# A decoder layer on one core: gates, scan output, half of h, queries, keys and probabilities transposed by DMA instead of on TensorE, and the weights of those stages loaded through GpSimd's queue

## The chip, the cores and the metric

The kernel runs on one core of one Trainium2 chip. The metric is the device time of one execution in microseconds; the number to beat is the median of three runs of the kernel before.

## The reference

One layer of a hybrid decoder for 256 tokens of width 2048, in float32. With n = RMSNorm of the stream at each place:

```
h = x + 1/2 * SwiGLU_1(RMSNorm(x))                     w_gu 2048 x 11264, w_down 5632 x 2048
P = RMSNorm(h) @ W_in                                  columns: u 2048 | v 2048 | z 2048 | x 2048 | B 1024 | C 1024 | dt 32
a = gelu(u) * (W_s RMSNorm(gelu(v)) + b)               causal within 128 tokens, 4 groups
m = RMSNorm(SSD scan(conv(x, B, C), dt) * silu(z))     32 heads of 64, state 128, chunks of 128
h = h + concat([a, m]) @ W_out                         4096 x 2048
h = h + softmax(q k^T / sqrt(512)) v @ W_o             4 heads; q from RMSNorm(h), k and v from RMSNorm(mem), 256 memory tokens
h = h + 1/2 * SwiGLU_2(RMSNorm(h))
out = RMSNorm(h)
```

Every matrix product on TensorE contracts over the partitions, so each activation that is produced with tokens on the partitions has to be transposed to features on the partitions before it can be the operand of the next product.

## The kernel before, in words

**Precision.** A float32 product is made of three products of a faster type: each operand is split into a high part (a cast on ScalarE) and a low part (the difference, on VectorE), and high*high, high*low and low*high are added up in PSUM. So each weight tile of 1 MB (256 rows by 1024 columns, four blocks of 128 by 512) is loaded into one of three `raw` buffers, cast to `hi` (L169, three buffers), subtracted to `lo` (L177, two buffers), and multiplied.

**Pieces.** A product runs over pieces of 256 contracted rows; one piece is one *step*. A piece of kind C takes 24 matmuls of 512 columns. A piece of kind S uses a scheme of the Strassen-Winograd kind with seven block products instead of eight, 21 matmuls, and more VectorE work (sums of the weight blocks, two splits). Its weights are loaded by three transfers (L151 once, L154 twice), those of a C piece by one (L140). Strings such as "CCSCSCSC" say which piece is of which kind; the first of `OUT_KINDS` holds the pieces of the gating operand `at`, the second those of the scan operand `mt`, and the output projection names for each half of its columns how they are multiplied. A slot of 8 KB per partition (12 in `big`) holds two C pieces or one S piece.

**Stages in order.** FFN 1 (up to about 640 us, its last down projection to about 700); the mix stage: B, C and x columns with features on the partitions (`proj_feat`), then v, u and z columns with tokens on the partitions (`proj_tok`), with the scan worked in between; the output projection in two halves of 1024 columns, 16 pieces each (`add_sum`, 1198 to 1365 us); queries for heads 0-1 and 2-3, keys, values (`heads`, 8 pieces for each pair of heads), the attention of each head (`attend`, `turn_probs`, `weigh`); the output of the attention (`add_sum`); FFN 2 from about 1750 us.

**Order of work.** TensorE keeps the order of the program. Jobs that prepare the next stage are put off by `later(fn, by)` and called at the first step at which they fall due; while all eight PSUM banks are taken (between the first and the last S piece), only jobs marked `bankless` are called. The other engines and the queues are ordered by a planner that goes by the code's order among what it reckons to be ready; `issue_after` (in `behind`, `in_turn`) holds some instructions in order on ScalarE and VectorE.

**Transposes.** Most operands are transposed on TensorE (`transpose`, L77): a block of 128 by 128 against the identity into a PSUM bank, eight for a chunk of 256 tokens by 512 columns, then cast and subtracted from the bank (`to_operand`, `Pieces.put`, `Pieces.sums`). This is done for the gates (`ats.later`), the scan output (`mts.later` in `m_operand`), the four chunks of h for the mix stage, the attention and FFN 2 (`Normed.chunk`), queries and keys (`by_head`), and the probabilities (`turn_probs`). The hidden units of both FFNs go another way (`Pieces.turn_later`): ScalarE copies a tile into planes of 16-bit halves (L485), GpSimd's queue writes them to device memory (L487), and SyncE's queue reads them back with a transposing transfer (L491) into a tile `turned` in SBUF, of which the operand is made.

**Queues.** All weights are loaded on SyncE's queue (`load`). GpSimd's queue carries the planes, the memory tokens (`prep_mem`, L1005 and L109), the decay rows of the scan, and small loads; GpSimd itself computes the power -1/2 of each norm (L361). Each queue is worked in order: an issue that waits holds those behind it.

Of the kernel before, what the change touches and what calls it, by code (L numbers as in the profile page):

```python
# [17 lines left out]
P = 128  # L18
D = 2048
S = 256  # L20
# [27 lines left out]
def hybrid_layer(ctx: ExitStack, tc: tile.TileContext, x, xt, mem, memt, w_gu1, w_dn1, w_in, w_s, w_out,  # L48
# [12 lines left out]
    tmp = ctx.enter_context(tc.tile_pool(name="tmp", bufs=6))  # L61
# [73 lines left out]

    def load(w, r0, cs, at, fine=False):
        raw = wraw.tile([P, 2 * KP, NC], F32, name="raw")
        rows = w[r0:r0 + KP * P, :]
        if at is PLAIN and cs[1] == cs[0] + NC:
            nc.sync.dma_start(out=raw.rearrange("p (k j) n -> p k j n", j=2), in_=rows[:, cs[0]:cs[0] + 2 * NC].rearrange(  # L140
                "(k p) (j n) -> p k j n", p=P, j=2))
            return raw
        if fine:
            for (k, j), b in at.items():
                nc.sync.dma_start(out=raw[:, b, :], in_=rows[k * P:(k + 1) * P, cs[j]:cs[j] + NC])
            return raw
        for j, c in enumerate(cs):
            b, e = at[0, j], at[1, j]
            src = rows[:, c:c + NC]
            if e > b:  # L150
                nc.sync.dma_start(out=raw[:, b:e + 1:e - b, :], in_=src.rearrange("(k p) n -> p k n", p=P))  # L151
                continue
            for k, x in enumerate((b, e)):
                nc.sync.dma_start(out=raw[:, x, :], in_=src[k * P:(k + 1) * P, :])  # L154
# [210 lines left out]
    def in_turn(src, last, op):  # L365

        if not src.tensor.name.startswith("turned"):
# [6 lines left out]
    def to_operand(srcs, dst, q, c0=None, of=None):  # L374
# [13 lines left out]
        else:  # L388
            scs = [col[:, c0 + of + k:c0 + of + k + 1] for k in range(2)]
            for k in range(2):  # L390
                hi = nc.scalar.activation(dst[:, q + k, :S], ps[:, k, :], AF.Copy, scale=scs[k])
            for k in range(2):
                lo = nc.vector.scalar_tensor_tensor(out=dst[:, q + k, S:], in0=ps[:, k, :], scalar=scs[k],
                                                    in1=dst[:, q + k, :S].bitcast(F32),
                                                    op0=ALU.mult, op1=ALU.subtract)
# [19 lines left out]

    owed = []


    class Pieces(dict):
        def __init__(self, kinds, name, donor=None):  # L420

            self.kinds, self.name, self.half, self.made, self.donor = kinds, name, None, {}, donor

# [33 lines left out]
        def sums(self, dst, ps, c0=None):  # L457
            in_sbuf = ps.tensor.name.startswith("turned")
            if not in_sbuf or c0 is not None:
                a = half_k(F32, "forms").rearrange("p (f s) -> p f s", f=4)  # L460
            if in_sbuf and c0 is None:
                a = ps
            elif c0 is None:
                nc.scalar.copy(out=a, in_=ps)
            else:
                for k in range(2):
                    nc.scalar.activation(a[:, 2 * k:2 * k + 2], ps[:, 2 * k:2 * k + 2], AF.Copy,
                                         scale=col[:, c0 + k:c0 + k + 1])

            b = half_k(F32, "forms").rearrange("p (f s) -> p f s", f=4)  # L470
            in_turn(a, last_split, lambda: nc.vector.tensor_tensor(
                out=b[:, 0:2], in0=a[:, 1:2].broadcast_to([P, 2, P]), in1=a[:, 0:4:3], op=ALU.subtract))
# [8 lines left out]
        def turn_later(self, srcs, by):  # L481
            planes = dram.tile([S, 2, NC], U16, name="planes", tag="planes", bufs=2)
            for t in range(NT):
                halves = tmp.tile([P, 2 * NC], U16, name="halves", tag="t2k")
                nc.scalar.copy(out=halves.rearrange("p (b n) -> p b n", b=2),  # L485
                               in_=srcs[t].bitcast(U16).rearrange("p (n b) -> p b n", b=2))
                nc.gpsimd.dma_start(out=planes[t * P:(t + 1) * P].rearrange("p b n -> p (b n)"), in_=halves)  # L487
            for q in (0, 2):
                def fetch(q=q):
                    to = half_k(F32, "turned").rearrange("p (k s) -> p k s", k=KP)  # L490
                    nc.sync.dma_start(out=to.bitcast(U16).rearrange("p k s -> p (k s)").rearrange("p (k s) -> p k s", k=KP),  # L491
                                      in_=planes[:, :, q * P:(q + 2) * P].rearrange("s b n -> (s b) n"), transpose=True)
# [700 lines left out]
```

## Time and profile before

| | |
|---|---|
| median of 3 runs | 2431.41 us (2431.26 to 2431.83) |
| the profiled execution | 2432.23 us, span 2430.5 us |
| TensorE (PE) | busy 2419.1 us, 100% |
| TensorE weight load (PEld) | 2014.9 us, 83% |
| VectorE (DVE) | 2033.1 us, 84% |
| ScalarE (ACT) | 1351.7 us, 56% |
| GpSimd (POOL) | 59.0 us, 2% |
| granted TensorE clock | 0.999 |
| moved by DMA | 503.87 MB, mean 207 GB/s |
| SyncE's queue (q1) | 475.86 MB, 60.6% of the 16 DMA engines' span |
| GpSimd's queue (q0) | 25.12 MB, 2.8% |

A row of a group has line, engine, operation, output<-input by the program's names with shapes, the count, then busy us and mean ns of one, and behind the next bar the idle time of the engine just ahead of these instructions with what ended it. A row of a wait has who waited, for whom, the us in total, how often, and the longest. "PE" is the matrix multiplication, "PEld" the loading of its stationary operand; SPq and POOLq are the queues of SyncE and GpSimd. A matmul's duration in a row is the pipelined one; the distance from one to the next is shorter.

### The profile page before, as it was taken

The numbers are of one execution on the slowest core, as the hardware profiler recorded it, in microseconds if no ns is written. First come the engines' busy times: TensorE is split into PE (matmuls) and PEld (weight loads), VectorE is DVE, ScalarE is ACT, GpSimd is POOL, SyncE is SP. The second block draws the span as 40 slices with busy tenths as digits, with TensorE's granted clock in tenths as the row PEclk, the third lists the DMA queues.
The fourth block names the chain that finished last, engine by engine and source line by source line (L and its number), as shares of the span: only waits on it lengthen the run. The fifth ranks groups of instructions, "written<-read, shape, count | busy, mean of one in ns | idle before, by whom it ended". The sixth has DMA issues, their size and how long they took to land.

```text
span 2430.5 us, 29042 instructions
## 1 busy us (share of the span) xinstructions
PE 2419.1 (100%) x11189; PEld 2014.9 (83%) x11189; DVE 2033.1 (84%) x1943; ACT 1351.7 (56%) x1251; POOL 59.0 (2%) x112
## 2 busy tenths in 40 slices
PE   9999999999999999999999999999999999999998
PEld 7888888888888888788888888888888888888887
DVE  8999889999877777655698888778899988899997
ACT  7565446565556555435555655555556554556554
POOL 1000000000000000000000000000000000000000
PEclk9999999999999999999999999999999999999999
DMA  8767667677555555545566655555567666776774
GB/s 302 238 221 232 205 208 232 221 232 227 196 186 189 189 185 179 204 160 187 182 203 231 232 187 165 174 182 181 187 213 240 225 213 203 223 226 226 232 220 154
DMA packets 251211, 503.87 MB, mean 207 GB/s; under 512 B 62896, under 2 KB 64976, under 8 KB 250304
## 3 DMA queue, kind: packets, MB, share of 16 engines
q1 hardware_dynamic: 243552, 475.86, 60.6%
q0 software_dynamic: 6688, 25.12, 2.8%
q8 instruction: 87, 1.43, 0.2%
q10 hardware_dynamic: 832, 1.05, 0.1%
q14 instruction: 52, 0.43, 0.1%
HBM read 476.76 MB, written 13.66 MB: 202 GB/s over the span
## 4 chain that ended last, share of the span: by engine, by line
PE 94%; issue 3%; DVE 1%; ACT 1%; DMA 0%; POOL 0%; SPq 0%; POOLq 0%; DVEq 0%; ACTq 0%
PE acc L74 91%; PE tpose L77 1%; PE yp L74 1%; PE o L74 0%; PE logits L74 0%; DVE lo L177 0%; ACT hi L169 0%; DVE sum L177 0%; PE mixed L74 0%; DMA raw<-in_w_gu 0%; PE dt L74 0%; DVE part L568 0%; PE scores L74 0%; PE yo L74 0%; PE st L74 0%
## 5 line engine op out<-in xcount | busy, mean ns | idle before, releaser
L177 DVE TENSOR_TENSOR lo<-raw,hi 128x2048 fp32r<-128x2048 f32 (+2 forms) x449 | 944.8, 2106 | 251.6 <-PE acc L74 194.7
L169 ACT CAST hi<-raw 128x2048 fp32r<-128x2048 f32 (+1 forms) x437 | 785.2, 1798 | 504.9 <-PE acc L74 447.1
L74 PE MATMUL acc<-hi,xp_ffn 128*128 128x512 f32 x1824 | 573.8, 389 | 0.0
L74 PEld LDWEIGHTS acc<-hi,xp_ffn 128*128 128x128 f32 x1824 | 342.3, 188 | 71.6 <-ACT hi L191 0.6
L169 ACT CAST hi<-sum 128x2048 fp32r<-128x2048 f32 x117 | 224.1, 1916 | 296.1 <-DVE sum L177 158.2
L74 PE MATMUL acc<-lo,xp_ffn 128*128 128x512 f32 x912 | 355.0, 389 | 1.4 <-DVE h L629 1.2
L177 DVE TENSOR_TENSOR lo<-sum,hi 128x2048 fp32r<-128x2048 f32 x117 | 268.1, 2291 | 36.7 <-ACT hi L169 36.7
L74 PE MATMUL acc<-hi,hid 128*128 128x512 f32 x896 | 281.9, 389 | 0.0
L74 PE MATMUL acc<-hi,xt_mix 128*128 128x512 f32 x768 | 242.6, 393 | 0.0
L74 PEld LDWEIGHTS acc<-lo,xp_ffn 128*128 128x128 f32 x912 | 171.2, 188 | 37.6 <-DVE h L629 1.6
L568 DVE TENSOR_TENSOR part<-acc,part 128x512 f32<-128x512 f32 x272 | 180.4, 685 | 24.1 <-PE acc L74 8.7
L74 PEld LDWEIGHTS acc<-hi,hid 128*128 128x128 f32 x896 | 168.2, 188 | 34.9
L74 PE MATMUL acc<-lo,hid 128*128 128x512 f32 x448 | 174.3, 389 | 0.0
L74 PEld LDWEIGHTS acc<-hi,xt_mix 128*128 128x128 f32 x768 | 144.2, 188 | 30.6 <-issue 1.0
L177 DVE TENSOR_TENSOR sum<-sum,raw 128x512 f32<-128x512 f32 x234 | 161.4, 690 | 6.2
L74 PE MATMUL acc<-lo,xt_mix 128*128 128x512 f32 x384 | 149.6, 390 | 0.0
L74 PE MATMUL acc<-hi,xp_ffn1s 128*128 128x512 f32 x466 | 148.5, 389 | 0.0
L74 PE MATMUL acc<-hi,xp_ffn2s 128*128 128x512 f32 x466 | 148.5, 389 | 0.0
L177 DVE TENSOR_TENSOR sum<-raw 128x1024 f32<-128x1024 f32 x117 | 142.4, 1217 | 0.4 <-DMA raw<-in_w_gu 0.4
L74 PE MATMUL acc<-xt_mix,hi 128*128 128x512 f32 x512 | 140.5, 396 | 0.0
L74 PE MATMUL acc<-hi,hids 128*128 128x512 f32 x392 | 125.2, 389 | 0.0
L74 PE MATMUL acc<-hi,memt 128*128 128x512 f32 x384 | 123.4, 392 | 0.0
(294 smaller groups left out, 3157.8 us busy)
## 6 DMA issues: line engine op xcount, KB each, us to landing
raw<-in_w_gu SPq DMA_DIRECT2D x284, 512.0 KB, 4.4
raw<-in_w_in SPq DMA_DIRECT2D x80, 1024.0 KB, 5.1
raw<-in_w_dn SPq DMA_DIRECT2D x60, 1024.0 KB, 5.1
raw<-in_w_gu SPq DMA_DIRECT2D x136, 256.0 KB, 4.7
raw<-in_w_kv SPq DMA_DIRECT2D x24, 1024.0 KB, 5.3
raw<-in_w_out SPq DMA_DIRECT2D x21, 1024.0 KB, 5.1
raw<-in_w_dn SPq DMA_DIRECT2D x28, 512.0 KB, 4.1
raw<-in_w_dn SPq DMA_DIRECT2D x56, 256.0 KB, 4.5
```

The costliest lines, as they stand in the source:

```text
L74: return pe(nc.tensor.matmul(out, lhsT=lhsT, rhs=rhs, start=start, stop=stop))
L77: return pe(nc.tensor.transpose(out=out, in_=in_, identity=identity))
L169: last_cast[:] = [nc.scalar.copy(out=t[:, :n], in_=x[:, :n]).ins]
L177: last_split[:] = [nc.vector.tensor_tensor(**kw).ins]
L568: nc.vector.tensor_tensor(out=out, in0=a, in1=b, op=op)
```

## The change

The transposes named in the title are made by transfers instead of on TensorE. `turn_later` is taken apart into `write_planes` (copies and writes), `read_turned` (the transposing read) and `turn_over` (write now, read at one due time, use at a second); `operand_turned` does this for operands that are not pieces. The gates, the scan output, chunks 0 and 1 of h for the mix stage and the attention, queries, keys and probabilities use them; chunks 2 and 3, and all of h for FFN 2, stay on TensorE. From the output projection until FFN 2, `queue` sends the weights through GpSimd's queue and the planes (and the memory tokens) through SyncE's. Due times are moved to fit (scan chunks two steps apart, `attend` at 7 instead of 2), `OUT_KINDS` holds other pieces as S with the same number of S pieces multiplied in each half, and the small tiles get a seventh buffer, into which the tile `idle` moves.

```diff
+    queue = {"weights": nc.sync, "planes": nc.gpsimd}
...
-            nc.sync.dma_start(out=raw.rearrange("p (k j) n -> p k j n", j=2), ...
+            queue["weights"].dma_start(out=raw.rearrange("p (k j) n -> p k j n", j=2), ...
...
-    def in_turn(src, last, op):
+    def write_planes(srcs, n=NC):
+        planes = dram.tile([len(srcs) * P, 2, n], U16, name="planes", tag="planes", bufs=4)
+        for t, src in enumerate(srcs):
+            halves = tmp.tile([P, 2 * n], U16, name="halves", tag="t2k")
+            nc.scalar.copy(out=halves.rearrange("p (b n) -> p b n", b=2),
+                           in_=src.bitcast(U16).rearrange("p (n b) -> p b n", b=2))
+            queue["planes"].dma_start(out=planes[t * P:(t + 1) * P].rearrange("p b n -> p (b n)"), in_=halves)
+        return planes
+
+    def read_turned(to, planes, c0, n):
+        nc.sync.dma_start(out=to, in_=planes[:, :, c0:c0 + n].rearrange("s b n -> (s b) n"), transpose=True)
+
+    def turn_over(srcs, by, put):
+        planes = write_planes(srcs)
+
+        def fetch(q):
+            to = half_k(F32, "turned")
+            read_turned(to.bitcast(U16).rearrange("p (k s) -> p k s", k=KP), planes, q * P, KP * P)
+            later(lambda: put(to.rearrange("p (k s) -> p k s", k=KP), q), by=by[1], bankless=True)
+
+        for q in (0, 2):
+            later(lambda q=q: fetch(q), by=by[0] + q / 4, bankless=True)
...
+    def operand_turned(srcs, to, name, c0=None, by=(1, 4)):
+        at = len(to) + sum(1 for o in owed if o is to)
+        owed.append(to)
+
+        def put(src, q):
+            if q == 0:
+                owed.remove(to)
+                assert len(to) == at
+                to.append(slot([P, KG, 2 * S], F32R, name))
+            to_operand(src, to[at], q, c0)
+
+        turn_over(srcs, by, put)
...
         def chunk(self, n, by=1):
             srcs = [h[n][:, t, :] for t in range(NT)]
-            if isinstance(self.xts, Pieces):
+            turned = n < 2 and self.name != "ffn2"
+            if turned and isinstance(self.xts, Pieces):
+                self.xts.turn_later(srcs, (2.5 + 1.5 * n, 2.5), self.c0 + n * KG, 2 * n)
+                later(lambda: self.stats(n), self.stats_by)
+            elif turned:
+                operand_turned(srcs, self.xts, f"xt_{self.name}{n}", self.c0 + n * KG, (2.5 + 1.5 * n, 2.5))
+                self.stats(n)
+            elif isinstance(self.xts, Pieces):
...
-    idle = const.tile([P, S], F32, name="idle")
+    idle = half_k(F32, "idle")[:, :S]
...
-    OUT_KINDS = "CCCCSCSC", "SCSCSCSC"
+    OUT_KINDS = "CCSCSCSC", "CCSCSCSC"
...
-            ats.later(gss[j], by=1 + j)
+            ats.turn_later(gss[j], (2.5 + 1.5 * j, 2.5))
...
-        mts.later(gs, C_SSM + c * KG)
+        mts.turn_later(gs, (1, 2.5), C_SSM + c * KG)
 
     for c in range(4):
-        later(lambda c=c: m_operand(c), by=1 + c)
+        later(lambda c=c: m_operand(c), by=1 + 2 * c, bankless=True)
...
-    add_sum(w_out, 0, Both(), ("CCCCCCSC" + OUT_KINDS[1], OUT_KINDS[0] + OUT_KINDS[1]), None, 1.0, na.chunk)
+    queue.update(weights=nc.gpsimd, planes=nc.sync)
+    add_sum(w_out, 0, Both(), ("CCCCSCSC" + OUT_KINDS[1], OUT_KINDS[0] + OUT_KINDS[1]), None, 1.0, na.chunk)
...
-            nc.gpsimd.dma_start(out=m_t.rearrange("p c n -> p (c n)"), in_=mem[t * P:(t + 1) * P, :])
+            queue["planes"].dma_start(out=m_t.rearrange("p c n -> p (c n)"), in_=mem[t * P:(t + 1) * P, :])
...
-                operand_later([got[j, 0], got[j, 1]], to, name, by=1 + j / 2)
+                operand_turned([got[j, 0], got[j, 1]], to, name, by=(1 + j / 4, 4))
...
-        later(lambda: turn_probs(hd, pr), by=1.5)
+        planes = write_planes([pr[:, t, :] for t in range(NT)], S)
+        later(lambda: turn_probs(hd, planes), by=1, bankless=True)
+
+    def turn_probs(hd, planes):
+        to = half_k(F32, "turned")
+        read_turned(to.bitcast(U16).rearrange("p (k s) -> p k s", k=KP), planes, 0, S)
+        later(lambda: split_probs(hd, to.rearrange("p (m s) -> p m s", m=2)), by=4, bankless=True)
...
-            later(lambda hd=hd + j: attend(hd, kts[hd]), by=2 + j / 2)
+            later(lambda hd=hd + j: attend(hd, kts[hd]), by=7 + j / 2)
...
+    queue.update(weights=nc.sync, planes=nc.gpsimd)
     ffn(n2, w_gu2, w_dn2, each=finish, by_token=True)
```

More of the change, by code (lines that the diff above doesn't have):

```diff
@@ L139, in load @@
         if at is PLAIN and cs[1] == cs[0] + NC:
-            nc.sync.dma_start(out=raw.rearrange("p (k j) n -> p k j n", j=2), in_=rows[:, cs[0]:cs[0] + 2 * NC].rearrange(
+            queue["weights"].dma_start(out=raw.rearrange("p (k j) n -> p k j n", j=2), in_=rows[:, cs[0]:cs[0] + 2 * NC].rearrange(
                 "(k p) (j n) -> p k j n", p=P, j=2))
@@ L144, in load @@
             for (k, j), b in at.items():
-                nc.sync.dma_start(out=raw[:, b, :], in_=rows[k * P:(k + 1) * P, cs[j]:cs[j] + NC])
+                queue["weights"].dma_start(out=raw[:, b, :], in_=rows[k * P:(k + 1) * P, cs[j]:cs[j] + NC])
             return raw
@@ L150, in load @@
             if e > b:
-                nc.sync.dma_start(out=raw[:, b:e + 1:e - b, :], in_=src.rearrange("(k p) n -> p k n", p=P))
+                queue["weights"].dma_start(out=raw[:, b:e + 1:e - b, :], in_=src.rearrange("(k p) n -> p k n", p=P))
                 continue
             for k, x in enumerate((b, e)):
-                nc.sync.dma_start(out=raw[:, x, :], in_=src[k * P:(k + 1) * P, :])
+                queue["weights"].dma_start(out=raw[:, x, :], in_=src[k * P:(k + 1) * P, :])
         return raw
@@ L362, in rstd_of, with in_turn @@
         return r
-    def in_turn(src, last, op):
-        if not src.tensor.name.startswith("turned"):
+    def write_planes(srcs, n=NC):
[16 more added lines that the diff above has]
+            later(lambda q=q: fetch(q), by=by[0] + q / 4, bankless=True)
+    def in_turn(src, last, op, c0=None):
+        if not src.tensor.name.startswith("turned") or c0 is not None and c0 < C_MIX:
             return op()
@@ L422, in __init__ @@
             self.kinds, self.name, self.half, self.made, self.donor = kinds, name, None, {}, donor
+            self.due = 0
         def add(self, srcs, q, c0):
@@ L458, in sums @@
             in_sbuf = ps.tensor.name.startswith("turned")
[L459 to L460 removed]
+            a = ps if in_sbuf else half_k(F32, "forms").rearrange("p (f s) -> p f s", f=4)
             if in_sbuf and c0 is None:
[L462 removed]
+                pass
             elif c0 is None:
@@ L479, in sums, with turn_later @@
             return hi.ins, lo.ins
[L481 to L492, printed above, removed]
-                    later(lambda: self.put(len(self), to, 0, None), by=by[1], bankless=True)
-                later(fetch, by=by[0] + q / 4, bankless=True)
+        def turn_later(self, srcs, by, c0=None, at=None):
+            if at is None:
+                at = self.due
+                self.due += 2
+            turn_over(srcs, by, lambda to, q: self.put(at + q // 2, to, q, c0))
         def later(self, srcs, c0=None, by=1):
@@ L1011, in prep_mem @@
             for i in range(4):
-                turned_load(memt, half * 4 + i, nc.gpsimd, two[:, i])
+                turned_load(memt, half * 4 + i, queue["planes"], two[:, i])
                 turned.append(two[:, i])
@@ L1074, in attend, with split_probs @@
             nc.vector.tensor_scalar(out=pr[:, t, :], in0=pr[:, t, :], scalar1=sm[:, t:t + 1], scalar2=None, op0=ALU.mult)
-        later(lambda: turn_probs(hd, pr), by=1.5)
-    def turn_probs(hd, pr):
-        tps = side("tpose").rearrange("p (m s) -> p m s", m=2)
-        for m in range(2):
-            for t in range(NT):
-                transpose(out=tps[:, m, t * P:(t + 1) * P], in_=pr[:, t, m * P:(m + 1) * P], identity=ident)
+        planes = write_planes([pr[:, t, :] for t in range(NT)], S)
[4 more added lines that the diff above has]
+        later(lambda: split_probs(hd, to.rearrange("p (m s) -> p m s", m=2)), by=4, bankless=True)
+    def split_probs(hd, tps):
         if hd % 2 == 0:
             pts.append(slot([P, 2, 2, 2 * S], F32R, "pts"))
-        split_to(pts[hd // 2][:, hd % 2], tps)
+        to_operand(tps, pts[hd // 2][:, hd % 2], 0)
     for hd in (0, 2):
```

19 lines of the change are left out of this document (10 added, 9 removed).

## The prediction

> **What bounds the kernel now.** I read the page's totals first, then the chain of work that ended last.
>
> ```profile
> span 2430.5 us, 29042 instructions
> PE 2419.1 (100%) x11189; PEld 2014.9 (83%) x11189; DVE 2033.1 (84%) x1943; ACT 1351.7 (56%) x1251; POOL 59.0 (2%) x112
> PE 94%; issue 3%; DVE 1%; ACT 1%; DMA 0%; POOL 0%; SPq 0%; POOLq 0%; DVEq 0%; ACTq 0%
> ```
>
> TensorE is busy for the whole span and carries 94% of the chain. The chain in order of time (start us, us, what), in the first FFN and in the first half of the output projection:
>
> ```profile
> 83.45 555.65 PE acc L74 x2450
> ...
> 1204.31 0.87 PE tpose L77 x8
> 1205.18 5.46 PE acc L74 x24
> ```
>
> The first FFN is one unbroken run of 2450 matmuls. In the output projection 24 matmuls of weights take 5.46 us (0.228 us each), and eight transposes push the next group back by 0.87 us: 0.109 us each, nothing beside them. A transpose taken away is time taken away, as long as TensorE finds its next operands ready. So the second question is how much the other engines have in hand. Busy time by stretch (us, PE busy, PEld, DVE, ACT, POOL, clock, DMA share, GB/s):
>
> ```profile
> 1198.00:1280.00 82.00, 82.00 (x380) 68.27 (x380) 75.43 (x82) 46.38 (x46) 0.00 (x0) 1.00 0.56 185
> 1280.00:1370.00 90.00, 90.00 (x411) 74.81 (x410) 77.40 (x68) 48.77 (x47) 6.91 (x10) 1.00 0.73 250
> ```
>
> TensorE has no gap in either; VectorE is the next engine, at 92% and 86%, and the DMA engines have a quarter to a half free. The granted clock is 1.00. Waits (us in total, times, longest): first the only one of TensorE's weight loads from 1198 to 1760 us.
>
> ```profile
> PEld acc L74 <- DVE lo L177: 0.2, 1, 0.2
> ```
>
> ScalarE in 1198 to 1280 us, its longest:
>
> ```profile
> ACT hi L169 <- PE acc L74: 25.7, 12, 4.2
> ```
>
> ScalarE in 1280 to 1370 us, where it waited for transfers:
>
> ```profile
> ACT hi L169 <- DMA raw<-in_w_q: 2.8, 1, 2.8
> ACT hi L169 <- DMA raw<-in_w_out: 2.1, 1, 2.1
> ```
>
> The cast that follows a weight load waits for TensorE to give a buffer back (25.7 / 12 = 2.1 us a time), so the weights mostly lie there already. Only beside the memory loads (1280 to 1370 us) were two weight loads waited for, by 2.1 and 2.8 us, and TensorE did not notice.
>
> **What is removed.** All transposes on TensorE, by source tile:
>
> ```profile
> L77 PE MATMUL tpose<-ident,h x96: 270/272/273, 638.9 to 1750.5; 128*128 128x128 f32 x96
> L77 PE MATMUL tpose<-ident,part x64: 270/272/273, 1405.7 to 1551.6; 128*128 128x128 f32 x64
> L77 PE MATMUL tpose<-ident,gate x32: 270/272/273, 1057.9 to 1110.3; 128*128 128x128 f32 x32
> L77 PE MATMUL tpose<-ident,y x32: 270/272/329, 1197.5 to 1217.6; 128*128 128x128 f32 x32
> L77 PE MATMUL tpose<-ident,probs x16: 272/272/273, 1530.0 to 1581.5; 128*128 128x128 f32 x16
> ```
>
> Gone are all of gate (32), y (32), part (64: queries and keys) and probs (16). Of h there are three consumers (mix, xa, ffn2) with 32 each; the change turns chunks 0 and 1 of mix and xa alone, so 16 + 16 = 32 go. Together 176. At 0.87 / 8 us each: 176 x 0.109 = 19.1 us. The 272 ns of a row are its pipelined length, not its share; I take the pitch. The number of weight matmuls does not change: the output projection has 5 and 6 S pieces in its two halves under the old and the new kinds alike.
>
> **What is added beside the path.** Each turned piece needs a de-interleaving copy on ScalarE and a write, then one transfer that turns two 128-column blocks. From the code: 8 + 8 + 8 + 16 + 8 = 48 copies and writes (gates, y, h, queries and keys, probabilities) and 8 + 8 + 8 + 16 + 4 = 44 turning transfers. The kernel does the same for its FFN hidden units, so there are rows:
>
> ```profile
> L485 ACT COPY halves<-part 128x1024 uint16<-128x1024 uint16 x44 | 45.9, 1043 | 45.6 <-DVE part L597 45.6
> L385 ACT CAST hid<-turned 128x512 fp32r<-128x512 f32 x28 | 17.2, 615 | 0.0
> ```
>
> Transfers (KB, us to landing), and SyncE's waits for a write before it can issue a turn:
>
> ```profile
> planes<-halves POOLq DMA_DIRECT2D x44, 256.0 KB, 4.5
> turned<-planes SPq DMA_TRANSPOSE x44, 3.9
> ```
>
> ```profile
> SPq L491 <- DMA planes<-halves: 26.8, 24, 2.9
> ```
>
> ScalarE gains 40 x 1.04 + 8 x 0.52 = 46 us over some 1100 us in which it is little over half busy: nothing on the path, as 82.00 - 46.38 = 36 us are free in the fullest stretch and at most 20 copies fall there. Its casts of operands are there before as after (615 ns each from a turned tile). A piece takes 1.04 + 4.5 + 3.9 = 9.4 us from copy to landing; the code asks for the turned tile 2.5 to 4 steps after the transfer's issue (a step is 4.8 to 5.5 us), that is 12 us at the least against 3.9 + 2.9 (the longest wait of SyncE for a write). Cost: 0. If that cover were gone, ScalarE would hold at that operand, and the weight casts behind it would be late next. The mix stage and the end of the first FFN keep weights and turns on SyncE, which the first FFN does in its unbroken run. Queries' and keys' operands, the attention of a head and its probabilities come some 5 steps later each than before, by their due times; by the code the split of a pair's probabilities then falls due 12 steps after its keys' projection, and their first use stands 17 steps after it, so this costs 0. The seventh small buffer and the idle tile moved into it add no instruction: 0.
>
> **What is moved.** In the output projection, queries, keys and values, and w_o, 32 + 16 + 32 + 16 = 96 weight pieces (27 of them S, three issues each; 69 C, one issue) go from SyncE's queue to GpSimd's; SyncE then carries writes, turns and the memory loads. Landing of such sizes by queue, and the rows of what follows a load (mean ns second):
>
> ```profile
> raw<-in_w_out SPq DMA_DIRECT2D x21, 1024.0 KB, 5.1
> dec<-cum_rows POOLq DMA_DIRECT2D x4, 1024.0 KB, 7.2
> memturned<-in_memt POOLq DMA_DIRECT2D x8, 256.0 KB, 6.0
> ```
>
> ```profile
> L109 POOL DMA_DIRECT2D memturned<-in_memt x8 | 5.8, 727 | 12.2 <-PE acc L74 12.2
> L169 ACT CAST hi<-raw 128x2048 fp32r<-128x2048 f32 x320 | 611.8, 1912 | 381.0 <-PE acc L74 342.8 <-issue 17.3 <-DVE part L568 6.6
> L177 DVE TENSOR_TENSOR lo<-raw,hi 128x2048 fp32r<-128x2048 f32 x320 | 732.1, 2288 | 239.3 <-PE acc L74 183.5 <-issue 53.6 <-ACT hi L169 1.7
> L177 DVE TENSOR_TENSOR lo<-raw,hi 128x1536 fp32r<-128x1536 f32 x117 | 205.0, 1752 | 11.3 <-PE acc L74 11.3
> L177 DVE TENSOR_TENSOR sum<-sum,raw 128x512 f32<-128x512 f32 x234 | 161.4, 690 | 6.2
> L177 DVE TENSOR_TENSOR sum<-raw 128x1024 f32<-128x1024 f32 x117 | 142.4, 1217 | 0.4 <-DMA raw<-in_w_gu 0.4
> ```
>
> No row shows a weight load from GpSimd. Bounds: as fast as SyncE's (0), or as slow as the 1 MB of dec, 7.2 - 5.1 = 2.1 us later; I take the second. Three raw buffers turn over in three steps. A C step is 24 and an S step 21 matmuls: 5.47 and 4.79 us, and the tightest three (S C S) take 15.0 us. A C buffer is held 7.2 + 1.91 + 2.29 = 11.4 us. An S buffer: three issues of up to 0.73, landing 6.0 after the last begins (2 x 0.73 + 6.0 = 7.5), sums 1.22 + 2 x 0.69 = 2.6, split 1.75: 11.8 us. Both fit, with 3.2 us or more over. So the later landing costs 0 on TensorE; each microsecond beyond that cover would cost up to 96 us.
>
> GpSimd itself issues 69 + 81 = 150 transfers of at most 0.73 us, 110 us of a stage of some 560 us. It also runs the norms' powers; in this queue, loads stand behind them. The order in its queue is not the order of the code:
>
> ```profile
> 682.19 0.79 POOL L905 DMA_DIRECT2D sum<-in_w_s  x1
> ...
> 703.01 0.72 POOL L361 TENSOR_TENSOR rstd_mix<-ms,neghalf 128x2 f32<-128x2 f32 x1 [15.51 <-DVE ms L360]
> ...
> 1318.81 0.58 POOL L1005 DMA_DIRECT2D mem<-in_mem  x1 [121.94 <-PE acc L74]
> ```
>
> L905 stands in the code far behind the power of rstd_mix and yet was issued first: what is ready by the planner's reckoning goes ahead. So first loads of w_out, whose buffers come free before the last gate, should not stand behind rstd_m. Three powers (m, xa, mem) fall into the stage; from below they cost 0, from above one step beyond the cover each, 3 x 5.5 = 16 us. I take 1 us for these and for SyncE's queue, where a memory load that waits for its buffer has turns behind it, nearer to 0 because the turns of h fall due 2.5 to 4.5 steps after the first half ends (1280 us), before the first memory load was issued (1318.81 us), and the queries' parts are there only at 1405.7 us.
>
> **Sum.** 2432.2 us (profiled execution: span 2430.5 and 1.7 around it) - 19.1 + 1 = 2414.1; the median of the runs shown is 0.8 us lower than that execution, so 2413.3 us. I forecast 2413.
>
> **The rivals.** *Part of it is lost again* (between 5 and 15 us come back as gaps): late loads behind a power, or VectorE. For it: VectorE is 92% busy in the first half of the output projection, and taking 4 transposes' groups away (3.5 us) leaves 78.5 us for 75.4 us of its work. If stage by stage only half came through there and in the next ones, 2431.4 - 19.1 / 2 = 2422. Against it: VectorE still fits, and its work is unchanged.
>
> *Nothing is won.* The 16 us of the upper bound above and the lost 3.5 us eat it: 2431.4 - 19.1 + 19.5 = 2432. It needs every one of them at its upper end.
>
> *Slower: GpSimd's issues stall while VectorE works.* Place: S pieces, three issues each. If each waits out the instruction VectorE is in, up to 2.29 us, an S buffer is held up to 11.8 + 6.9 = 18.7 us against 15.0, and 27 pieces lose 3.7 us each: 100 us, 2512. At 1.6 us an issue it is 11.8 + 4.8 - 15.0 = 1.6 us, 43 us in all: 2455, the time I give it. It turns to slower from (19.1 / 27 + 3.2) / 3 = 1.3 us an issue. Against it: 727 ns for the memturned issue while VectorE was 86% busy in that stretch. The Trainium skill, page "SBUF — State Buffer", section "Who interferes with whom", has such a lock: VectorE's two-port modes (copies, casts, tensor_scalar) keep GpSimd from writing descriptors, and VectorE instructions with two SBUF inputs hold up GpSimd's reads but not its mere writes. By that rule the subtractions that fill VectorE here would not lock the issues out, and the 727 ns row agrees; if they did, the rival above is what it would cost.
>
> **How the numbers follow.** Forecast 0.64 (2409 to 2417); part lost 0.13; nothing won 0.09; slower 0.14. About 0.2%, 4.9 us, is what a measurement of this kernel can tell from no change, so the first two are faster: 0.77, then 0.09 and 0.14. The low end, 2409, is the ceiling (2412.3) with some 3 us in hand, should operands from SBUF ease a place; the high end has to take in part lost and some of nothing won: 2430.
>
> **What would show it.** Right: 106 transposes left on TensorE instead of 282, its span without new idle time, and ScalarE's casts still mostly ended by TensorE. Wrong: TensorE or its weight loads waiting for lo or hi from 1198 to 1760 us, with casts ended by a raw load of w_out, w_q, w_kv or w_o; landings over 10 us on GpSimd's queue; issues there of over 1.3 us.

## The result, and the profile after

The changed kernel takes 2461.51 us (median of 4 runs, 2460.4 to 2463.22) where the kernel before takes 2431.47 us beside it: a ratio of 1.0124 (95% interval 1.0109 to 1.0139), 30 us slower. The forecast was 2413 us.

The totals of the page after:

```profile
span 2458.7 us, 28930 instructions
PE 2411.5 (98%) x11013; PEld 2002.5 (81%) x11013; DVE 2033.6 (83%) x1944; ACT 1392.4 (57%) x1296; POOL 156.9 (6%) x264
PE 91%; DMA 3%; DVE 2%; ACT 2%; issue 1%; SPq 1%; POOL 0%; POOLq 0%; DVEq 0%; ACTq 0%
```

TensorE has 11013 matmuls instead of 11189: the 176 transposes are gone. But its busy time fell by only 7.6 us, not by 19.1, and the span has 47 us without it instead of 11. Transfers, which carried nothing of the chain before, now carry 3% of it. TensorE's waits after (us in total, times, longest), where before no line was over 1.3 us:

```profile
PE acc L74 <- DVE lo L179: 18.6, 11, 6.1
PE acc L74 <- ACT hi L171: 10.3, 2, 6.0
PE idle L74 <- DVE idle L671: 9.4, 1, 9.4
```

**Where the time went.** Three marks stand in the chain of both kernels: transposes of the third chunk of h for the mix stage, the same for the attention, and the long run of FFN 2 (start us, us, what). Before:

```profile
703.61 0.87 PE tpose L77 x8
1364.48 0.87 PE tpose L77 x8
1750.73 49.47 PE acc L74 x218
```

After:

```profile
707.31 0.87 PE tpose L77 x8
1371.19 0.87 PE tpose L77 x8
1778.59 665.79 PE acc L74 x2937
```

With the transposes taken out at 0.109 us each, 16 (1.75 us) ahead of the first mark, 80 (8.72 us) between the first two and 80 behind, the stretches should have become 701.86, 652.15 and 377.53 us long. They are 707.31, 663.88 and 407.40. So the start lost 5.4 us, the stretch with the output projection 11.7, queries to attention 29.9: 47.0 us over the ceiling of 2412.3 (2431.4 less the 19.1 us of the 176 transposes) make 2459; the marks are of one execution, which took 2460.4 us. FFN 2 takes the same time in both. The gates' part is not among the losers: from 707 to 1190 us TensorE is busy throughout in both kernels.

**What the waits look like.** ScalarE's waits for transfers from 1190 to 1600 us, where it had two before, 4.9 us in all:

```profile
ACT hi L171 <- DMA raw<-in_w_out: 16.0, 7, 5.0
ACT kt L410 <- DMA turned<-planes: 14.7, 6, 4.5
ACT mt L416 <- DMA turned<-planes: 8.4, 2, 5.7
ACT qt L410 <- DMA turned<-planes: 8.4, 2, 6.6
ACT pts L410 <- DMA turned<-planes: 5.7, 1, 5.7
```

They are 53.2 us, with some smaller rows 63.1; 37.2 of the 53.2 are for turned tiles. The first in ScalarE's timeline (start us, us, line, operation, idle time before it and what ended it):

```profile
1206.45 1.99 ACT L371 COPY halves<-y 128x1024 uint16<-128x1024 uint16 x2
1214.17 1.72 ACT L416 ACTIVATE mt<-turned,col 128x256 fp32r<-128x256 f32 x4 [5.73 <-DMA turned<-planes]
1215.80 3.26 ACT L171 CAST hi<-raw 128x2048 fp32r<-128x2048 f32 x2
```

and TensorE at the same place:

```profile
1213.03 0.39 PE L74 MATMUL acc<-hi,ats 128*128 128x512 f32 x1
1217.73 0.79 PE L74 MATMUL acc<-hi,at 128*128 128x512 f32 x1 [4.31 <-ACT hi L171]
1220.05 0.79 PE L74 MATMUL acc<-lo,at 128*128 128x512 f32 x1 [1.53 <-DVE lo L179]
1225.34 0.63 PE L74 MATMUL acc<-lo,at 128*128 128x512 f32 x1
```

These seven rows show the mechanism at one place. TensorE does not need `mt` here: it is working on pieces of the gates' operand (`ats` and `at`) and goes on doing so after the gap. But the cast that makes `mt` stands in ScalarE's order ahead of two casts of weights that TensorE does need. The turned tile comes 5.73 us late, ScalarE holds, the weights lie there uncast, TensorE stops for 4.3 us and once more for the split. The turn had been issued at 1208.03 us; ScalarE was ready for its tile at 1208.44 us.

The windows show a second price (us, PE busy, PEld, DVE, ACT, POOL, granted clock, DMA share, GB/s):

```profile
1215.00:1220.00 5.00, 0.79 (x1) 0.29 (x1) 3.70 (x6) 5.00 (x7) 0.00 (x0) 0.57 0.62 138
1220.00:1225.00 5.00, 4.95 (x12) 3.88 (x13) 4.58 (x5) 3.27 (x4) 1.17 (x2) 0.50 0.79 228
1500.00:1600.00 100.00, 88.12 (x399) 71.99 (x398) 68.76 (x65) 58.45 (x60) 14.86 (x23) 0.94 0.76 209
```

After the gap the clock is granted at 0.50: a matmul lasts 0.63 to 0.79 us instead of 0.39, and 12 of them fill 5 us. That is "busy", which is why the busy time hides part of the loss. The same happens behind the longest gaps in the attention, at a mean clock of 0.94 over the 100 us from 1500.

The turned tiles themselves, 1190 to 1600 us (issues, then landing):

```profile
L377 SPq DMA_TRANSPOSE turned<-planes x30: 1225/1490/5887, 1208.0 to 1583.7; - x30
DMA to landing us min/median/max: 3.5/6.7/14.4
```

In the kernel before, a turn lands after 3.4/4.0/7.1 us.

And the start. VectorE before, then after:

```profile
0.95 0.27 DVE L634 MEMSET idle<- 128x256 f32 x1
```

```profile
7.03 2.05 DVE L179 TENSOR_TENSOR lo<-raw,hi 128x512 fp32r<-128x512 f32 x3 [0.74 <-ACT hi L193]
9.08 0.27 DVE L671 MEMSET idle<- 128x256 f32 x1
```

The tile `idle`, moved into the pool of small buffers, is cleared only at 9.08 us, behind four splits of weights. TensorE could begin with these, but it keeps the program's order, and ten matmuls on `idle` stand first in it.

### The profile page after: what moved, and what is told of

It reads as the page before. It is cut to its first block, busy times and chain, and to the rows that moved or that the text cites. A ratio compares the mean times of both kernels' runs of the same rounds, so it can differ in the third digit from the quotient of the medians.

```text
span 2458.7 us, 28930 instructions
## 1 busy us (share of the span) xinstructions
PE 2411.5 (98%) x11013; PEld 2002.5 (81%) x11013; DVE 2033.6 (83%) x1944; ACT 1392.4 (57%) x1296; POOL 156.9 (6%) x264
## 4 chain that ended last, share of the span: by engine, by line
PE 91%; DMA 3%; DVE 2%; ACT 2%; issue 1%; SPq 1%; POOL 0%; POOLq 0%; DVEq 0%; ACTq 0%
PE acc L74 87%; DMA turned<-planes 2%; DMA planes<-halves 1%; DVE lo L179 1%; SPq L377 1%; ACT hi L171 1%; DVE sum L179 1%; PE yp L74 1%; ACT halves L371 0%; PE logits L74 0%; PE tpose L77 0%; PE o L74 0%; PE mixed L74 0%; DMA raw<-in_w_gu 0%; PE dt L74 0%
```

## The experiments

The kernel of reference in each comparison is the kernel before, 2431.5 to 2431.7 us beside all of them. Theory (A) after the profile: the exchange of queues makes turns land later, ScalarE's order passes the delay on to the weights. Rivals: the due times are merely too tight whatever the queue; the weights through GpSimd's queue are late in themselves; the number of turns in these stages is too much for any order.

### The idle tile in its own slot

```diff
-    idle = half_k(F32, "idle")[:, :S]
+    idle = slot([P, S], F32, "idle")
```

> The tile idle is taken out of the small tiles' buffers again (it gets a slot of the large pool, free at the start); all else is as in the changed kernel. Theory 1 (the start was lost to this tile: its memset stood behind VectorE's first splits, 9.08 us instead of 0.95 us): the warming matmuls start near 1.3 us again and the first FFN ends 5.4 us earlier: 2461.5 - 5.4 = 2456 us. Rival (the late start is made up for by the first FFN, and the 3.7 us at its end come from the turned chunks of h): no change, 2461 us.

Measured 2460.14 us (2455.53 to 2466.46), ratio 1.0118 (1.01 to 1.0136). TensorE's waits:

```profile
PE acc L74 <- DVE lo L179: 20.2, 12, 5.8
PE acc L74 <- ACT hi L171: 14.8, 3, 9.4
PE idle L74 <- DVE idle L671: 1.3, 1, 1.3
```

The wait at the start is gone (9.4 to 1.3 us) and the first mark stands at 701.07 instead of 707.31 us: the move alone costs about 6 us there. But the median gained only 1.4, where theory 1 named 5.4; in this execution the waits later were 6.1 us longer (35.0 against 28.9). Once ScalarE and the queues run late, what they lose differs from one execution to the next: these runs spread over 11 us.

### The queues not exchanged

```diff
-    queue.update(weights=nc.gpsimd, planes=nc.sync)
...
-    queue.update(weights=nc.sync, planes=nc.gpsimd)
```

> The two lines that exchange the queues are left out: weights stay on SyncE's queue and planes on GpSimd's for the whole kernel; turned tiles are as in the changed kernel. Theory A (the turned tiles are asked for too early by the due times, because ScalarE works some two pieces ahead of TensorE; the queue matters little): the gaps stay, 2450 us or more. Theory B (transposing transfers are slow because weights now come through another queue and share the 16 DMA engines with them): landing of the transposing transfers goes back from a median of 6.7 us in this stage to about 4, most of the 41 us of gaps after 1190 us go, about 2420 to 2425 us.

Measured 2436.69 us (2433.93 to 2439.01), ratio 1.0021 (1.0011 to 1.003). 24.8 of the 30 us are gone, with all 176 blocks still turned by transfers. The landing went back as theory B said; the time stayed above the 2420 to 2425 us that it named. Landing of the turned tiles from 1190 to 1600 us, and the marks in the chain:

```profile
DMA to landing us min/median/max: 3.0/4.5/8.9
```

```profile
1366.38 0.87 PE tpose L77 x8
1754.85 665.79 PE acc L74 x2937
```

The late landings have gone, and with them the wait for `hi`; the longest wait of TensorE but the one for `idle` is 1.8 us, and in this execution the clock is never at half. The first mark stands at 707.07 us; the stretches lose 5.2 (the idle tile), 7.2 and 10.9 us. What is still lost may come from the other side of the trade. SyncE's queue here:

```profile
1411.38 7.97 SPq L377 DMA_TRANSPOSE turned<-planes  x4
1419.44 0.53 SPq L153 DMA_DIRECT2D raw<-in_w_q  x1
```

Four turns take 8 us to issue, the waits for their planes among it, and the three issues of an S piece's weights stand behind them.

### Queries, keys and probabilities back on TensorE

```diff
-                operand_turned([got[j, 0], got[j, 1]], to, name, by=(1 + j / 4, 4))
+                operand_later([got[j, 0], got[j, 1]], to, name, by=1 + j / 2)
...
-            later(lambda hd=hd + j: attend(hd, kts[hd]), by=7 + j / 2)
+            later(lambda hd=hd + j: attend(hd, kts[hd]), by=2 + j / 2)
```

`turn_probs` is that of the kernel before; the exchange of queues stays.

> Queries, keys and probabilities are transposed on TensorE again (with their old due times); gates, scan output and half of h stay turned by transfers, queues exchanged as in the changed kernel. From the two traces the attention stages lose 29.9 us gross and win 8.7 us (80 transposes): 2461.5 - 29.9 + 8.7 = 2440 us if their turns are the cause (theories A and B alike). If instead the weights through GpSimd's queue were the cause of these gaps, they stay: about 2470 us.

Measured 2440.72 us (2436.93 to 2445.73), ratio 1.0037 (1.0025 to 1.0049). So the turning of these 80 blocks, meant to gain 8.7 us, costs 20.8 us with the queues exchanged. It takes both to make most of the loss: without the exchange or without these turns, 20 to 25 us are gone.

### A later use for the scan output's turned tiles

```diff
-        mts.turn_later(gs, (1, 2.5), C_SSM + c * KG)
+        mts.turn_later(gs, (1, 4.5), C_SSM + c * KG)
```

> Only the second due time of the scan output's turned tiles is moved, from 2.5 to 4.5 steps after the issue. Theory A: the gap of TensorE at 1213 to 1220 us and the half clock behind it go, up to 11.7 us: about 2450 us. Theory B: the transfers are slow, not early; the wait moves but some of it stays: 2455 us or more.

Measured 2466.0 us (2462.14 to 2467.26), ratio 1.0138 (1.0122 to 1.0153): no better. ScalarE's and TensorE's waits from 1190 to 1290 us:

```profile
ACT halves L371 <- DMA planes<-halves: 10.6, 2, 7.6
PE acc L74 <- ACT hi L171: 6.9, 1, 6.9
```

The wait for the turned tile is gone, as intended, and another has taken its place: the next copies into planes wait for a small buffer whose write has not landed, and the weights' casts stand behind those. The due time was too tight, but moving one does not help where ScalarE's next instruction depends on the same slow transfers.

### The exchange alone

The kernel before, with nothing more turned and the idle tile as it was.

```diff
+    queue.update(weights=nc.gpsimd, planes=nc.sync)
     add_sum(w_out, 0, Both(), ...
...
+    queue.update(weights=nc.sync, planes=nc.gpsimd)
     ffn(n2, w_gu2, w_dn2, each=finish, by_token=True)
```

> The kernel before, with nothing turned anew; only the weights from the output projection to the last product before FFN 2 go through GpSimd's queue, and the memory loads through SyncE's. If the weights through GpSimd's queue cost nothing by themselves (the prediction's step), the time is the kernel before's, 2431.5 us within 2 us. If they are the cause by themselves, it is 10 us or more above.

Measured 2435.39 us (2434.27 to 2436.63), ratio 1.0016 (1.0006 to 1.0026): 3.8 us, between the two values expected. Landing of w_out (KB, us), and TensorE's one wait over 1.3 us:

```profile
raw<-in_w_out POOLq DMA_DIRECT2D x21, 1024.0 KB, 5.6
```

```profile
PE tpose L77 <- DVE y L981: 2.6, 1, 2.6
```

The weights of w_out land 0.5 us later than through SyncE's queue (5.1 us before), those of w_kv 0.4 (5.7 and 5.3), and no cast of ScalarE waits for a transfer from 1190 to 1600 us. So the weights are not late in themselves. By the marks (702.62 and 1366.26 us here), 2.8 of the 3.8 us are lost between the first two, and this wait for `y` is where: VectorE scales `y` by the norm only after a split of weights (from 1198.69 us, with the norm's power begun on GpSimd at 1195.18), in the kernel before ahead of that split (1196.90 and 1196.16). The exchange changes VectorE's order there. The changed kernel has the same order: its first copy into planes starts at 1200.37 us, without the exchange at 1197.88, so its first turned tile is late by this too.

### The planes on GpSimd's queue too

```diff
-    queue.update(weights=nc.gpsimd, planes=nc.sync)
+    queue.update(weights=nc.gpsimd)
```

> The changed kernel with the planes written by GpSimd's queue all through, behind the weights there; SyncE's queue then holds nothing but the turns and the memory loads. If the turns land late because they stand in one queue with their own writes, their landing falls from 6.7 us to about 4 and 10 us or more are won (2450 us or less). If they land late because the weights run in another queue at the same time, landing stays at 6 to 7 us and the time at 2461 us or above.

The memory tokens go with the planes, so they are on GpSimd's queue here too, other than the expectation has it. Measured 2483.31 us (2477.73 to 2488.22), ratio 1.0212 (1.0196 to 1.0229), the slowest of all. Landing of the turned tiles from 1190 to 1600 us:

```profile
DMA to landing us min/median/max: 3.5/8.9/23.3
```

SyncE's queue holds nothing but turns in these stages, and they land later still: it is not their own writes in the same queue that make them late. Nor are the writes late on GpSimd's queue: each is issued at most 1.4 us after its copy, and they land after 5.1 us, as in the changed kernel (5.2). Why it is slower than the change is not shown.

### The mix stage alone

Gates and the mix stage's h turned (48 blocks), everything behind it, the idle tile and the queues as in the kernel before.

```diff
-            turned = n < 2 and self.name != "ffn2"
+            turned = n < 2 and self.name == "mix"
...
-        mts.turn_later(gs, (1, 2.5), C_SSM + c * KG)
+        mts.later(gs, C_SSM + c * KG)
```

> Only the gates and half of the mix stage's h are turned by transfers; scan output, queries, keys, probabilities and the attention's h stay on TensorE, queues as in the kernel before, the tile idle in a slot of its own. The stages up to 1190 us showed no gap in either trace, so the 48 transposes taken away come through: 2431.5 - 48 x 0.109 = 2426.3 us.

Measured 2427.27 us (2426.83 to 2428.67), ratio 0.9983 (0.9974 to 0.9993). 48 x 0.109 = 5.2 us would make 2426.4: 4.3 of them come through. The pitch and the mechanism of the prediction hold there, where weights and turns stay on one queue and at most one group of turns is under way. Such a group is of four turns for the gates. It holds SyncE's queue for 8.2 and 9.3 us (from 1060.81 and 1104.38 us), and TensorE has no wait: a group of four alone does not make a loss. The loads behind it are of C pieces here, one issue each.

### All turned, set further apart

All 176 blocks, queues not exchanged, idle tile in its own slot; turns and uses further apart (an argument for the distance of the two turns of a chunk is added, here one per step).

```diff
-        mts.turn_later(gs, (1, 2.5), C_SSM + c * KG)
+        mts.turn_later(gs, (1.5, 3, 2), C_SSM + c * KG)
...
-                self.xts.turn_later(srcs, (2.5 + 1.5 * n, 2.5), self.c0 + n * KG, 2 * n)
+                self.xts.turn_later(srcs, (2 + 2 * n, 3, 2), self.c0 + n * KG, 2 * n)
...
-                operand_turned([got[j, 0], got[j, 1]], to, name, by=(1 + j / 4, 4))
+                operand_turned([got[j, 0], got[j, 1]], to, name, by=(2 + 2 * j, 2.5, 2))
...
-            later(lambda hd=hd + j: attend(hd, kts[hd]), by=7 + j / 2)
+            later(lambda hd=hd + j: attend(hd, kts[hd]), by=9 + j / 2)
```

> All turns of the change, weights on SyncE and planes on GpSimd throughout, idle in a slot of its own, and the turns spread: reads one step apart and 1.5 to 2 steps after their writes (scan output 1.5 and 2.5, h of the attention 2, 3, 4, 5, queries and keys 2, 3, 4, 5), attention of a head at 9. Theory (without the swap, the weights of an S piece stand behind bursts of up to four turns and their waits for writes, 8 to 10 us of SyncE's queue): single turns with their writes landed hold the queue 1.3 us, the gaps go, 2412 to 2418 us. Rival (the turns are slow next to the weights wherever they stand, or ScalarE waits for them): gaps of 10 us or more stay, 2422 us or above.

Measured 2423.32 us (2421.37 to 2425.75), ratio 0.9967 (0.9956 to 0.9979): faster than the kernel before, by 8.3 us where 19.1 would be the ceiling, and above the 2412 to 2418 us that the theory named; the time is the rival's. The marks:

```profile
701.85 0.87 PE tpose L77 x8
1360.19 0.87 PE tpose L77 x8
1743.32 665.79 PE acc L74 x2937
```

The stretches lose 0, 6.2 and 5.6 us. In the kernel with the mix stage alone the middle stretch is 657.3 us long (702.87 to 1360.16); here it is 658.3. So of the 48 blocks of scan output and h that differ, worth 5.2 us, nothing is left. ScalarE's longest waits there are for weights:

```profile
ACT hi L171 <- DMA raw<-in_w_out: 23.5, 6, 7.3
```

Turns still go out in groups of three or four, since the planner orders SyncE's queue by its own reckoning; the due times moved the uses, not all of the issues.

### The exchange again, with all set further apart

```diff
+    queue.update(weights=nc.gpsimd, planes=nc.sync)
     add_sum(w_out, 0, Both(), ...
...
+    queue.update(weights=nc.sync, planes=nc.gpsimd)
```

> The kernel of the run before this one in the list of edits (all pieces turned, turns and uses set further apart, idle tile in its own slot), with one thing put back: weights of the output projection, queries, keys, values and w_o through GpSimd's queue, planes through SyncE's. With it the four corners are there: exchanged and tight 2460, not exchanged and tight 2437, not exchanged and far apart 2423, this one exchanged and far apart. Theory A (the exchange makes each turn land later, median 6 to 7 us and some over 10, and no setting of due times covers that): 2440 us or more, landing of turns at median 6 or more, TensorE waiting over 12 us in all for casts and splits between 1190 and 1600 us, with a granted clock of 0.5 behind the longest. Theory B (the due times alone were too tight; with more room the later landing is covered): 2420 to 2428 us, waits as without the exchange (8 us or less in all), no half clock, even if the landing stays at 6 us.

Measured 2442.01 us (2434.91 to 2444.94), ratio 1.0038 (1.0024 to 1.0052). Theory A named 2440 or more and half clock behind the longest wait; TensorE's longest wait, behind which the clock falls (mean 0.92 from 1190 to 1280 us), and the landing (1190 to 1600 us):

```profile
PE acc L74 <- ACT hi L171: 8.7, 1, 8.7
```

```profile
DMA to landing us min/median/max: 3.2/6.5/14.8
```

So the exchange costs 18.7 us here and 24.8 us at the tight settings, and the landing goes from 5.4 (all set further apart, without the exchange) to 6.5 and from 4.5 to 6.7 us. The wider settings help with the exchange too (18.1 us against the run with the idle tile in its own slot, 2460.14), but do not cover it. The losses by the marks of one execution each, worked out as above, beside the median time; in both tight kernels the start has the idle tile among the first operands:

| | start | to the attention's h | to FFN 2 | median us |
|---|---|---|---|---|
| exchanged, tight (the change) | 5.4 | 11.7 | 29.9 | 2461.51 |
| not exchanged, tight | 5.2 | 7.2 | 10.9 | 2436.69 |
| exchanged, further apart | -0.6 | 16.7 | 11.4 | 2442.01 |
| not exchanged, further apart | 0.0 | 6.2 | 5.6 | 2423.32 |

### Turned: mix stage, queries, keys and probabilities

All set further apart, without the exchange, but scan output and the attention's h on TensorE.

```diff
-            turned = n < 2 and self.name != "ffn2"
+            turned = n < 2 and self.name == "mix"
...
-        mts.turn_later(gs, (1.5, 3, 2), C_SSM + c * KG)
+        mts.later(gs, C_SSM + c * KG)
```

> Turned by transfers: gates, mix's h, queries, keys, probabilities (far apart); y and xa's h stay on TensorE; queues not exchanged, idle tile in its own slot. 128 of the 176 transposes are gone: 128 x 0.109 = 14.0 us. Theory A (each stage pays for itself; the attention gains what it gained in the kernel with all turned, 3.1 us, and output projection and xa's queries go as in the kernel before): 2427.3 - 3.1 = 2424. Theory B (in the attention the loss of 5.6 us came over from the y and h turns ahead of it, whose loads and casts were late): the full 8.7 us, 2418.6. At 2422 or less B carries most of it; at 2424 or more A.

Measured 2423.15 us (2422.22 to 2424.17), ratio 0.9966 (0.9952 to 0.9979): as fast as all turned, with 48 blocks fewer. By its time it lies between the two theories; the marks decide. From the attention's h to FFN 2:

```profile
1358.33 0.87 PE tpose L77 x8
...
1740.66 665.79 PE acc L74 x2937
```

382.3 us, against 386.3 with the mix stage alone and 383.1 with all turned: it loses 4.8 of 8.7 us by itself; at most 0.8 of the 5.6 us came over from the stage ahead. SyncE's queue at one place:

```profile
1494.83 0.53 SPq L153 DMA_DIRECT2D raw<-in_w_kv  x1
1495.46 4.27 SPq L377 DMA_TRANSPOSE turned<-planes  x2
1499.79 1.05 SPq L156 DMA_DIRECT2D raw<-in_w_kv  x2
```

Two turns, 4.3 us with their waits, stand between the first and the other two loads of one S piece, and the sums of its weights need all three.

### The exchange in FFN 2 alone

The kernel before, queues exchanged in FFN 2 only, whose 22 turns between 1775 and 2400 us come two at a time.

```diff
+    queue.update(weights=nc.gpsimd, planes=nc.sync)
     ffn(n2, w_gu2, w_dn2, each=finish, by_token=True)
```

> The kernel before, nothing more turned than there, with the queues exchanged in the second FFN alone: its weights through GpSimd's queue, the planes of its hidden units through SyncE's, its turns on SyncE's as before. In the kernel before this stretch (1775 to 2400 us) is one unbroken run, one column group's turns at a time, landing 3.5/3.9/7.1 us (min, median, max), no wait of TensorE. What is disputed is why turns land later in the changed kernel's attention. Theory A (the exchange by itself: turns on one queue and weights on another share the 16 DMA engines, and whatever is dense there only adds): the landing of the turns in the second FFN rises to a median of 5 us or more with a maximum over 9; since the uses stand four steps (some 20 us) behind, little of it reaches TensorE: 2432 to 2445. Theory B (the number of turns and writes at one time in the attention and the output projection makes it, not the exchange): landing stays at a median of 4.5 or less and a maximum of about 7, TensorE without waits: 2430 to 2434.

Measured 2431.7 us (2431.61 to 2432.07), ratio 1.0001 (0.9991 to 1.001). Transfers from 1775 to 2400 us, and their landing:

```profile
planes<-halves SPq DMA_DIRECT2D x22, 256.0 KB, 3.5
turned<-planes SPq DMA_TRANSPOSE x22, 5.0
```

```profile
DMA to landing us min/median/max: 3.3/5.0/7.6
```

Before, in the same stretch, it was 3.5/3.9/7.1 us. Both theories got half: the exchange by itself adds 1.1 us to a turn's landing, but the longest hardly grows, and with uses four steps behind TensorE sees nothing of it. Landings of 12 us and more were seen only where the exchange meets the denser stages behind the mix stage (12.8 us in the output projection with queries and keys on TensorE again); which of their turns, writes and memory loads makes it was not separated.

## Why the prediction was wrong, step by step

**Right: the ceiling's size and the mix stage.** 176 transposes left TensorE, at the pitch taken: with the mix stage alone, 4.3 of 5.2 us come through. Weights through GpSimd's queue were bounded at 2.1 us later and cost nothing by the sum; with nothing turned beside them they land 0.4 to 0.5 us later, and the exchange alone costs 3.8 us.

**Wrong first: "Cost: 0" for the turned tiles.** This step failed, and most of the loss goes with it: 20 to 25 of the 30 us are gone without the exchange or without the turns of the attention. It set a cover of 12 us (2.5 steps from the turn's issue to the tile's use) against 3.9 + 2.9 us, both from stages with two turns at a time. Neither side held. The steps are TensorE's; ScalarE came to the twelve turned tiles that it had to wait for between 1190 and 1600 us only 0.4 to 10.3 us after their turns were issued. At the first of them it was early without the exchange too (3.6 us after the issue, and held there for 3.55 us), so at these tiles the 12 us were not there. And in the changed kernel a turn lands after 6.7 us in the middle and 14.4 at the longest, and the writes on SyncE's queue take 5.2 us instead of 4.5. The prediction named what would follow ("ScalarE would hold at that operand, and the weight casts behind it would be late next") and set its price to 0, as it compared the due time with a median landing and one wait from quieter stages. It is what happened: 63 us of ScalarE's waits for transfers instead of 4.9, of them some 37 for turned tiles and 22 for weights. That the operand is needed on TensorE many steps later is no cover. What counts is where the cast stands in ScalarE's order.

**Wrong second: "The mix stage and the end of the first FFN keep weights and turns on SyncE, which the first FFN does in its unbroken run" was taken as good for the rest.** The stages behind it were costed by the loads alone: three raw buffers, 3.2 us in hand. ScalarE held for 5.7 us by a turned tile is more than that, and a raw buffer that stays full holds the next load too.

**Wrong third: the idle tile, "adds no instruction: 0".** It adds none, but moves one in VectorE's order, and TensorE's first matmuls wait for it: 5 to 6 us.

**Not costed: the clock.** That TensorE would come back from a gap at half clock stands nowhere in the prediction, since no gap of that length was in the profile before.

**The rivals.** The slower one put the loss on issues of GpSimd stalled by VectorE. The trace refutes that mechanism: its issues of weights last 0.54 to 0.78 us, under the 1.3 us at which that rival began. It had the side right for a reason that did not occur. The time of "part lost" (2422) is near where the same turns end without the exchange, set further apart: 2423.32. Among the signs named, "casts ended by a raw load", "TensorE waiting for lo or hi" and "landings over 10 us on GpSimd's queue" came true, the last for four of 150 loads (11.9 us at the longest); issues of over 1.3 us did not. The longest landings were those of turns on SyncE's queue (14.4 us).

**How the loss of 49 us divides** (2461.5 less the ceiling of 2412.3): 24.8 go with the exchange (2461.5 less 2436.7); 13.4 with the idle tile and the tight settings (2436.7 less 2423.3), of which the marks give 5.2 to the idle tile; 11.0 are left even with all set further apart and no exchange. The marks put these last on the output projection (6.2) and the attention (5.6), and the rows show loads behind groups of turns in SyncE's queue. That these groups are the cause is argued, not shown: whether another order of that queue would win the 11 us was not tried. The first two shares depend on each other, as the table shows: with the settings further apart the exchange costs 18.7.

**Why turns land later beside weights on another queue.** The mean load does not tell: from 1480 to 1590 us the DMA engines are busy 0.79 and 0.78 of the time with the exchange (tight, further apart) and 0.74 and 0.79 without it, in FFN 2 0.69 and 0.70. What tells is the moment of the turn. Between a turn's issue and its landing the engines are fully busy either way (in FFN 2 0.99 of the time before and 1.07 with the exchange there, where 1 is all 16 engines; medians of 22 turns). The turns' own packets take the same time of them (2.8 and 2.7 us), but the larger packets that start meanwhile (2 KB and more, mostly weights) carry 1.02 MB instead of 0.43 and take 2.8 us of the engines instead of 1.2. From 1190 to 1600 us it is 1.14 MB in the changed kernel and 0.48 without the exchange. So a turn with the weights on another queue shares the full engines with more weights, and lands later. That in one queue these weights stand behind the turn is the likely reason, but is not shown by itself. Open is what makes the longest landings.

The Trainium skill, page "DMA: Bandwidth & Descriptors", section "Issuing engines are not separate DMA queues", has transfers of all issuing engines interleave on the same 16 DMA engines, so that a second queue saves issue time only. The runs agree as far as they go: with the exchange in FFN 2 the planes landed faster (4.6 to 3.5 us), the 256 KB loads of w_gu a little (4.6 to 4.3), but the 1 MB loads (5.1 to 5.6) and the turns (3.9 to 5.0) later.

## What to carry to other kernels

An operand that is brought by a transfer must be there not when TensorE needs it but when the engine that casts it reaches it in its order, with everything behind that cast counted as late too; count the cover from where that engine will be, not in steps of TensorE, and set it against the longest landing in that stage, not against a median from a quieter one. Moving loads to a second queue takes them from behind the turns, but here the turns then landed later; with the present code it was better to leave them on one queue and set the turns apart, and to turn only where the stage has room: mix stage, queries, keys and probabilities, 2423.15 us against 2431.68 (ratio 0.9966, 0.9952 to 0.9979), which is as good as turning all. A small tile that the first matmuls wait for should not share buffers with the first operands.

## What the runs showed of the hardware

**The clock after a gap.** In the kernel before the clock is 1.00 in every stretch looked at. After TensorE's gap from 1213.4 to 1217.7 us it was granted 0.57 and then 0.50, and matmuls lasted 0.63 to 0.79 us. Only from about 1226 us on were they back at 0.39. In the 5.3 us from 1220.05 to 1225.34 us 12 matmuls started, at 0.44 us each instead of 0.227: a gap of 4 us cost, by this, nearly 3 us more behind it. Without the exchange, where no wait of TensorE but the first one at the start is over 1.8 us, the clock stays at 1.00 in these stages of the profiled execution. The Trainium skill, page "TensorE: Matmul & The Clock Gate", section "HAM oscillation — how this bites in real kernels", describes it: a wait for data that crosses the activity window brings the clock to half and the next work starts cold. The trace agrees.

**Landing beside another queue.** A turn of 256 KB lands 1.1 us later in the middle (3.9 to 5.0 us) when the weights beside it go through GpSimd's queue instead of its own, in a stage that is otherwise the same and at the same share of the DMA engines (0.70 and 0.69). The loads of 1 MB take 5.6 us instead of 5.1. While such a turn is under way the engines are full in both, and 1.02 MB instead of 0.43 pass in packets larger than its own.
